# Hybrid encoder block on one core: pooling's products as the mixer's first projections, value convolutions between the retention heads, z gates behind them

## Chip, cores, metric

One core of a Trainium2 chip. The metric is the device time of one launch in microseconds; several runs of a kernel give a median. The engines are TensorE (PE in the rows; PEld is its weight load), VectorE (DVE), ScalarE (ACT), GpSimd (POOL) and SyncE (SP, which issues the weight transfers).

## What is computed

Two layers, each a token mixer and a SwiGLU feed-forward, on 512 tokens of width 1024. The mixer projects the normalised input and feeds three branches:

```python
qkv = silu(causal_depthwise_conv(dn_qkv, dn_conv))          # q, k, v of the delta rule, 4 heads
o_dn = gated_delta_rule(l2(q), l2(k), v, beta, g)           # chunks of 64, state carried over 8 chunks
o_dn = rms(o_dn) * dn_out_norm * silu(dn_z)                 # the z gate
o_pool = einsum(trailing_mean(u, (2, 4, 8, 16)) - u, pool_w) * pool_scale
o_ret = group_norm(chunkwise_retention(rq, rk, rv)) * ret_out_norm * silu(ret_g)
y = gate0 * (o_dn @ w_branch_dn) + gate1 * (o_pool @ w_branch_pool) + gate2 * (o_ret @ w_branch_ret)
x = x + rms_norm(y @ w_out);  then the feed-forward
```

`g` and `beta` (the token gates) come from a narrow projection of eight columns.

## The kernel before

Activations lie transposed: 128 channels on the partitions, 512 tokens along the row. Every float32 product is made from rounded halves: `weights` loads a 128 x 1024 weight block by SP, `split1` cuts each half of it into a high part on ACT (L232, `wh`) and a low part on DVE (L233, `wl`), and `mm3` (L222 to L224) adds three matmuls. A projection (`project`) is thus 24 matmuls of 512 columns, and a branch product of `w_branch_*` 12. The input norm's factor `rb` is not known when the first products of a stage run, so each projection's result is multiplied by `rb` when it leaves PSUM.

At a stage's start four projections run while the stage before is being finished (`begin`, `hand_over`); which four is said by `first_of_mixer`: in the kernel before the four key projections. Their PSUM tiles are the list `firsts`.

The mixer itself consists of one long chain and of filler. The chain is `delta()`: token gates (L505 to L570; its matmuls are L514, L520 and L567), transposed keys (L689), decays from GpSimd sums (L709, L710, matmuls L717, L718), Gram matrices (L737, L740), a forward solve of 15 small DVE steps, two block levels (`back`), eight chunk steps that carry the state (L800, L815, L837), norm and output. The filler is the list `tasks`: generators that each give one projection or branch product in pieces; whenever the chain yields n, `fill(n)` runs n pieces of the first task and a piece of `side` (retention's `attention`). `need(key)` runs tasks until a convolution is there.

A framework then orders each engine's instructions by its own estimate of when they are ready, so that the order below is what counts, not the order of the code. Each engine works its list in order.

Task order before: convolutions of the four keys from `firsts`; `pooled` 0 to 3, each with its projection; query convolutions with `pool_map` and the first two branch products of pooling (`p(0)`, `p(1)`) between them; each value convolution with one `p(n)`; retention heads 0 and 1, `p(6)`, heads 2 and 3, `p(7)`; eight branch products of retention. The z gates' projections are run by the chain itself at its end (L858). The branch of the delta rule and `w_out` follow in the tail.

`pooled(gi)` multiplies the projection by `rb` on DVE (L959, tile `u`), then adds shifted copies on GpSimd (L965; gi + 1 adds for window 2 to the power gi + 1, ten in all), and subtracts on DVE (L969, L973, L976). Its tiles, like those of the convolutions, gates and the retention, come from one tag `ft` of four buffers:

```python
        def ft():
            return tl("ft", FT, (P, S + 16))
```

Of the kernel before, what the change touches and what calls it, by code (L numbers as in the profile page):

```python
# [9 lines left out]
F32 = mybir.dt.float32  # L10
F32R = mybir.dt.float32r
# [7 lines left out]
P = 128  # L19
# [113 lines left out]
def tile_hybrid(ctx: ExitStack, tc: tile.TileContext, x_in, consts, rot, rmask, vecs, wab, wi, wpl, wbr, wo, wgu, wd, out):  # L133
# [325 lines left out]
        return dst, hs, rb, pss  # L459

    def first_of_mixer(l):
        return vec[:, l, V_PRE1 : V_PRE1 + KT], [wi[l, B_K + h] for h in range(H)]

    def first_of_ffn(l):
        return vec[:, l, V_PRE2 : V_PRE2 + KT], [wgu[l, 0, 0], wgu[l, 0, 1], wgu[l, 1, 0], wgu[l, 1, 1]]
# [15 lines left out]
    def mixer(l, xd, hs, rb, firsts):  # L481
# [17 lines left out]


        tok = {}

        def token_gates():
            raw = tl("mc", 2, (P, NT * B16))
            nc.scalar.dma_start(out=raw, in_=wab[l])  # L505
            abw = keep.tile([P, D], F32R, tag="wq", bufs=H, name=nm("abw"))
            G.memset(abw.bitcast(F32), 0.0)
            r8, w8 = raw.rearrange("p (k n) -> p k n", n=8), abw.rearrange("p (k n) -> p k n", n=P)
            V.tensor_copy(out=w8[:, :, 0:8], in_=r8)
            V.tensor_tensor(out=w8[:, :, 8:16], in0=r8, in1=w8[:, :, 0:8].bitcast(F32), op=ALU.subtract)  # L510
            ps = psum_f()
            for k in range(KT):
                for j in range(2):
                    T.matmul(ps, lhsT=w8[:, k], rhs=hs[k][j], start=k == 0 and j == 0, stop=k == KT - 1 and j == 1)  # L514
            yield
            ab = tl("ft", FT, (P, S + 16))
            V.tensor_tensor(out=ab[0:16, 0:S], in0=ps[0:16], in1=rb[0:16], op=ALU.mult)
            pst = psum_o()
            for t in range(NT):
                T.matmul(  # L520
                    pst[:, t * 8 : t * 8 + 8], lhsT=ab[0:16, ts(t)], rhs=kc[0:16, K_SEL : K_SEL + 8], start=True, stop=True
                )
            yield
            abt = pst[:, 0:32].rearrange("p (t n) -> p n t", n=8)

            beta = tiny("beta")
            A.activation(out=beta.rearrange("p (n t) -> p n t", n=4), in_=abt[:, 0:4], func=AF.Sigmoid)
            sx = tiny("sx")
            V.tensor_tensor(
                out=sx.rearrange("p (n t) -> p n t", n=4),  # L530
                in0=abt[:, 4:8],
                in1=vec[:, l, V_DTB : V_DTB + 16].rearrange("p (n t) -> p n t", n=4),
                op=ALU.add,
            )

            nab = tiny("nab")
            V.scalar_tensor_tensor(out=nab, in0=sx, scalar=-1.0, in1=sx, op0=ALU.mult, op1=ALU.min)
            e = tiny("e")
            A.activation(out=e, in_=nab, func=AF.Exp)
            ea = tiny("ea")  # L540
            A.activation(out=ea, in_=vec[:, l, V_ALOG : V_ALOG + 16], func=AF.Exp)
            den = tiny("den")
            V.tensor_scalar(out=den, in0=e, scalar1=2.0, scalar2=None, op0=ALU.add)
            V.reciprocal(out=den, in_=den)
            yield
            z = tiny("z")
            V.tensor_tensor(out=z, in0=e, in1=den, op=ALU.mult)
            z2 = tiny("z2")
            V.tensor_tensor(out=z2, in0=z, in1=z, op=ALU.mult)
            po = tl("po", 2, (P, 16))  # L550
            V.tensor_scalar(out=po, in0=z2, scalar1=2.0 / 17, scalar2=None, op0=ALU.mult)
            for c in (15, 13, 11, 9, 7, 5, 3):
                po2 = tl("po", 2, (P, 16))
                V.scalar_tensor_tensor(out=po2, in0=po, scalar=2.0 / c, in1=z2, op0=ALU.add, op1=ALU.mult)
                po = po2
            yield
            lp = tiny("lp")
            V.scalar_tensor_tensor(out=lp, in0=po, scalar=2.0, in1=z, op0=ALU.add, op1=ALU.mult)
            sp = tiny("sp")
            V.scalar_tensor_tensor(out=sp, in0=sx, scalar=0.0, in1=lp, op0=ALU.max, op1=ALU.add)  # L560
            g = tiny("g")
            V.scalar_tensor_tensor(out=g, in0=sp, scalar=-1.0, in1=ea, op0=ALU.mult, op1=ALU.mult)
            for _ in range(GATES):
                yield
            pcs = psum_c()
            for n, m in enumerate((c_le, c_gt, c_e0, c_e1)):
                T.matmul(pcs[:, n * 16 : n * 16 + 16], lhsT=m, rhs=g, start=True, stop=True)  # L567
            yield
            ex = tiny("ex", 64)
            A.activation(out=ex, in_=pcs[:, 0:64], func=AF.Exp)  # L570
            tok.update(beta=beta, g=g, e_g=ex[:, 0:16], e_tail=ex[:, 16:32], e_last=[ex[:, 32:48], ex[:, 48:64]])
            yield
# [1 line left out]

        wq = [keep.tile([P, 3 * S], F32, tag="wq", bufs=H, name=nm("wq")) for _ in range(H)]
        w4 = [t.rearrange("p (t s c) -> p t s c", t=NT, s=6) for t in wq]

        ku = tl("ku", 1, (P, H * S))  # L580
        k4 = ku.rearrange("p (h t v) -> p h t v", h=H, t=NT)
# [59 lines left out]
                done.add(key)  # L641
                yield

        def conv_first():
            for h, ps_ in enumerate(firsts):
                conv(ps_, 4 + h, ("k", h))
                yield

        def z_gate(h):
            res = []  # L650
            yield from project(wi[l, B_Z + h], hs, res)
            t = tl("ft", FT, (P, S + 16))[:, 0:S]
            V.tensor_tensor(out=t, in0=res[0], in1=rb, op=ALU.mult)
            sg = tl("ft", FT, (P, S + 16))[:, 0:S]
            A.activation(out=sg, in_=t, func=AF.Sigmoid)
            o = tl("c1", 4)
            V.scalar_tensor_tensor(out=o, in0=t, scalar=vec[:, l, V_DN : V_DN + 1], in1=sg, op0=ALU.mult, op1=ALU.mult)
            return o

        def square_sums(src, v, h):  # L660
            sq = tl("c1", 4)
# [12 lines left out]
                V.tensor_copy(out=out[ROWS[f]], in_=src[ROWS[1 - f]])  # L674
            return out

        os_ = []

        def delta():
            half = (P, NT * C)  # L680
# [174 lines left out]
            V.tensor_tensor(out=rt, in0=r, in1=rqw, op=ALU.mult)  # L855
            yield WAITS["norm"]
            for h in range(H):
                zg = yield from z_gate(h)  # L858
                on = tl("c1", 4)
                scaled(on, hs_of(ku, h), rt[:, hc(h)])  # L860
                yield WAITS["on"]
                ps = psum_c()
                transposed(on, ps)
                od = tl("ft", FT, (P, S + 16))[:, 0:S]
                for f in range(2):
                    a, b = slice(f * C, (f + 1) * C), slice((1 - f) * C, (2 - f) * C)
                    V.tensor_tensor(out=hd(od)[:, :, a], in0=hd(ps)[:, :, b], in1=hd(zg)[:, :, a], op=ALU.mult)
                os = keep.tile([P, 2 * S], F32R, tag="wq", bufs=H, name=nm("os"))
                split1(od, os[:, 0:S], os[:, S:])
                os_.append((os[:, 0:S], os[:, S:]))  # L870
# [80 lines left out]
        mixes = {}  # L951

        def pooled(gi):
            res = []
            yield from project(wi[l, B_PU + gi], hs, res)
            win, pad = 2 ** (gi + 1), 16
            u = ft()
            G.memset(u[:, 0:pad], 0.0)
            V.tensor_tensor(out=u[:, pad:], in0=res[0], in1=rb, op=ALU.mult)  # L959
            src, first = u, 0  # L960
            for a in range(gi + 1):
                d = 2**a
                first += d
                t = ft()
                G.tensor_tensor(out=t[:, first:], in0=src[:, first:], in1=src[:, first - d : S + pad - d], op=ALU.add)  # L965
                src = t
            tag = ("kr", "qr", "vc", "mask")[gi]
            mixed = tl(tag)
            V.scalar_tensor_tensor(  # L969
                out=mixed[:, 16:], in0=src[:, pad + 16 :], scalar=1.0 / win, in1=u[:, pad + 16 :], op0=ALU.mult, op1=ALU.subtract  # L970
            )
            t = tl("pc", 1, (P, 16))
            V.tensor_tensor(  # L973
                out=t, in0=src[:, pad : pad + 16], in1=kc[:, K_CNT + 16 * gi : K_CNT + 16 * gi + 16], op=ALU.mult
            )
            V.tensor_tensor(out=mixed[:, 0:16], in0=t, in1=u[:, pad : pad + 16], op=ALU.subtract)  # L976
            mixes[gi] = mixed
            yield

        def pool_map(gi):  # L980
            mixed = mixes[gi]
# [134 lines left out]
            return [branch(i, name, gb, n) for n in range(a, b)]  # L1116

        def convs(what, h):
            b, ch = {"q": (B_Q, 0), "v": (B_V, 8)}[what]
            return [conv_one(b + h, ch + h, (what, h))]  # L1120

        def p(n):
            return branches(0, "p", B_GA + 8, n, n + 1)

        side = []
        tasks = [conv_first()] + [pooled(i) for i in range(4)]
        tasks += convs("q", 0) + [pool_map(0), pool_map(1)] + convs("q", 1) + [pool_map(2), pool_map(3)]
        tasks += convs("q", 2) + p(0) + convs("q", 3) + p(1)
        for h in range(H):
            tasks += convs("v", h) + p(2 + h)  # L1130
        tasks += [retention(0), retention(1)] + p(6) + [retention(2), retention(3)] + p(7)
        tasks += branches(1, "r", B_GA + 16, 0, 8)

        def fill(n):
# [230 lines left out]
```

## Time and profile before

| | |
|---|---|
| median of 3 runs | 1900.73 us (1898.32 to 1903.97) |
| the profiled execution | 1900.81 us, span 1898.9 us |
| granted clock, mean over the span | 0.987 of 2.4 GHz |
| PE busy | 1834.2 us (97%) |
| DVE / ACT / POOL busy | 1041.6 (55%) / 701.0 (37%) / 395.4 us (21%) |
| chain that ended last | PE 82%, DVE 12%, ACT 2% |

Busy time of a matmul on PE overlaps that of the next. The engine lines tell how much of the span an engine worked; the 40 slices and the view by stretches tell where it did not; the timeline says of each gap on PE which engine's instruction ended it. Where PE has nothing else to do, a gap on PE is time.

### The profile page before, as it was taken

The page shows a single profiled execution, that of the slowest core. Times are in us where ns is not written, and L with a number is a line of the kernel's source. Part 1 is how long each engine was busy: PE and PEld are TensorE (multiplying, and loading weights), DVE is VectorE, ACT ScalarE, POOL GpSimd, SP SyncE. Part 2 cuts the span into 40 slices and gives each one's busy share as a digit, 9 for nine tenths or more (in the row PEclk, how much of TensorE's full clock was granted, in tenths as well). Part 3 has the DMA queues.
Part 4 walks back from the last instruction along what each step waited for, and adds up shares of the span by engine and source line. Part 5 has one row for each costly group of instructions (what it writes and reads, how often), then busy time and mean ns, then how long its engine had stood idle before and what let it go on. Part 6 is the DMA issues. An engine that isn't in the chain of part 4 may idle for free.

```text
span 1898.9 us, 24790 instructions
## 1 busy us (share of the span) xinstructions
PE 1834.2 (97%) x9286; PEld 1537.4 (81%) x9286; DVE 1041.6 (55%) x1973; ACT 701.0 (37%) x1251; POOL 395.4 (21%) x370
## 2 busy tenths in 40 slices
PE   7899999999999999999998999999999999999997
PEld 6677888778888888888976788887788988888887
DVE  6886476654438432343487965766544474324443
ACT  5533333233344332333354333332333443323332
POOL 2602010111223220222226020011122232102212
PEclk9899999999999999999998999999999999999999
DMA  6131112224325333223231211222243252333231
GB/s 203 45 95 59 56 59 81 92 79 144 99 67 182 98 100 100 93 96 100 79 129 45 85 58 59 66 81 92 78 144 100 78 178 91 98 100 99 91 100 45
DMA packets 65415, 177.70 MB, mean 94 GB/s; under 512 B 15376, under 2 KB 18448, under 8 KB 65296
## 3 DMA queue, kind: packets, MB, share of 16 engines
q1 hardware_dynamic: 54016, 172.78, 27.9%
q10 hardware_dynamic: 11280, 3.34, 0.8%
q8 instruction: 73, 1.20, 0.3%
q14 instruction: 46, 0.38, 0.1%
HBM read 167.18 MB, written 8.39 MB: 92 GB/s over the span
## 4 chain that ended last, share of the span: by engine, by line
PE 82%; DVE 12%; ACT 2%; issue 2%; ACTq 1%; DMA 1%; POOL 1%; SPq 0%; DVEq 0%; POOLq 0%
PE pp L222 24%; PE pp L223 24%; PE pp L224 24%; DVE wl L233 2%; DVE ct L610 1%; ACTq L782 1%; DVE hl L229 1%; PE cx L815 1%; PE cx L898 1%; DVE xt L329 1%; PE cx L908 1%; PE cx L800 1%; PE fx L498 1%; PE fx L267 1%; PE cx L498 0%
## 5 line engine op out<-in xcount | busy, mean ns | idle before, releaser
L232 ACT ACTIVATE wh<-raw 128x512 fp32r<-128x512 f32 x584 | 364.5, 628 | 726.7 <-PE pp L223 677.9
L222 PE MATMUL pp<-hh,wh 128*128 128x512 f32 x1568 | 624.1, 398 | 0.0
L223 PE MATMUL pp<-hl,wh 128*128 128x512 f32 x1568 | 615.5, 393 | 0.0
L224 PE MATMUL pp<-hh,wl 128*128 128x512 f32 x1568 | 614.0, 392 | 0.0
L233 DVE TENSOR_TENSOR wl<-raw,wh 128x512 fp32r<-128x512 f32 x584 | 416.3, 716 | 328.0 <-ACT wh L232 310.2
L222 PEld LDWEIGHTS pp<-hh,wh 128*128 128x128 f32 x1568 | 296.2, 189 | 62.6 <-issue 2.5
L224 PEld LDWEIGHTS pp<-hh,wl 128*128 128x128 f32 x1568 | 295.6, 189 | 62.2 <-issue 0.3
L223 PEld LDWEIGHTS pp<-hl,wh 128*128 128x128 f32 x1568 | 296.2, 189 | 59.6 <-issue 1.5
L222 PE MATMUL pp<-ah,wh 128*128 128x512 f32 (+1 forms) x418 | 149.1, 357 | 0.0
L224 PE MATMUL pp<-ah,wl 128*128 128x512 f32 (+1 forms) x418 | 148.6, 356 | 0.0
L223 PE MATMUL pp<-al,wh 128*128 128x512 f32 (+1 forms) x418 | 148.5, 356 | 0.0
L1244 POOL TENSOR_TENSOR gs<-gt,sg 128x512 f32<-128x512 f32 x44 | 56.6, 1287 | 314.3 <-ACT sg L1242 314.3
L1249 POOL TENSOR_TENSOR a<-gs,ut 128x512 f32<-128x512 f32 x44 | 70.4, 1601 | 135.9 <-DVE ut L1247 135.6
L289 POOL TENSOR_TENSOR sqa<-sqa,sq 128x256 f32<-128x256 f32 (+1 forms) x69 | 62.6, 907 | 127.4 <-ACT sq L282 108.1
L224 PEld LDWEIGHTS pp<-ah,wl 128*128 128x128 f32 x418 | 78.9, 189 | 11.4
L222 PEld LDWEIGHTS pp<-ah,wh 128*128 128x128 f32 x418 | 78.9, 189 | 11.4
L223 PEld LDWEIGHTS pp<-al,wh 128*128 128x128 f32 x418 | 79.0, 189 | 11.2
L233 DVE TENSOR_TENSOR al<-a,ah 128x512 fp32r<-128x512 f32 x44 | 31.3, 711 | 77.7 <-ACT ah L232 77.5
L610 DVE SCALAR_TENSOR_TENSOR ct<-ft,vec,ct 128x512 f32<-128x512 f32 x72 | 58.3, 810 | 9.0 <-ACT ct L607 7.9
L222 PE MATMUL pp<-yh,wh 128*128 128x256 f32 (+1 forms) x192 | 61.4, 320 | 0.0
L1247 DVE TENSOR_TENSOR ut<-pp,rb 128x512 f32<-128x512 f32 x42 | 29.0, 690 | 58.7 <-PE pp L224 58.7
L224 PE MATMUL pp<-yh,wl 128*128 128x256 f32 (+1 forms) x192 | 61.1, 318 | 0.0
(297 smaller groups left out, 2382.4 us busy)
## 6 DMA issues: line engine op xcount, KB each, us to landing
raw<-in_wi_dram SPq DMA_DIRECT2D x117, 512.0 KB
raw<-in_wgu_dram SPq DMA_DIRECT2D x88, 512.0 KB
raw<-in_wd_dram SPq DMA_DIRECT2D x44, 512.0 KB
raw<-in_wbr_dram SPq DMA_DIRECT2D x24, 512.0 KB
raw<-in_wo_dram SPq DMA_DIRECT2D x16, 512.0 KB
xd<-xt SPq DMA_DIRECT2D x24, 256.0 KB
xt<-xd SPq DMA_DIRECT2D x24, 256.0 KB
xt<-in_x_dram SPq DMA_DIRECT2D x16, 256.0 KB
```

The lines of the kernel that those rows point to most:

```text
L222: T.matmul(ps, lhsT=w[0], rhs=m[0], start=start, stop=False)
L223: T.matmul(ps, lhsT=w[0], rhs=m[1], start=False, stop=False)
L224: T.matmul(ps, lhsT=w[1], rhs=m[0], start=False, stop=stop)
L229: V.scalar_tensor_tensor(out=lo, in0=src, scalar=scalar, in1=hi.bitcast(F32), op0=ALU.mult, op1=ALU.subtract)
L232: A.activation(out=hi, in_=src, func=AF.Copy)
L233: V.tensor_tensor(out=lo, in0=src, in1=hi.bitcast(F32), op=ALU.subtract)
L267: T.matmul(ps[:, t : t + 1], lhsT=sq[:, ts(t)], rhs=one, start=i == 0, stop=i == len(sqs) - 1)
L289: G.tensor_tensor(out=t, in0=acc[0], in1=acc[1], op=ALU.add)
L610: V.scalar_tensor_tensor(out=a2, in0=u[:, j : j + S], scalar=tap(j), in1=a, op0=ALU.mult, op1=ALU.add)
L1244: G.tensor_tensor(out=gs, in0=gt, in1=sg, op=ALU.mult)
L1247: V.tensor_tensor(out=ut, in0=up, in1=rb, op=ALU.mult)
L1249: G.tensor_tensor(out=a, in0=gs, in1=ut, op=ALU.mult)
```

## The change

`first_of_mixer` names the four pooling projections, and `pooled` becomes a plain function that takes them from `firsts` and runs four times before the tasks begin. Keys are projected and convolved as tasks, `pool_map` and the eight branch products of pooling stand between key and query convolutions (the last one behind the first value convolution), and the value convolutions stand between the retention heads. The z gates become tasks behind the retention; their outputs are kept in four buffers that are free by then, and the chain waits for them by `need`. The tile `abw` is taken first from its tag, and the four `wq` tiles when they are first used. No arithmetic is changed.

```diff
     def first_of_mixer(l):
-        return vec[:, l, V_PRE1 : V_PRE1 + KT], [wi[l, B_K + h] for h in range(H)]
+        return vec[:, l, V_PRE1 : V_PRE1 + KT], [wi[l, B_PU + g] for g in range(4)]
...
         tok = {}
+        abw = keep.tile([P, D], F32R, tag="wq", bufs=H, name=nm("abw"))
...
-            abw = keep.tile([P, D], F32R, tag="wq", bufs=H, name=nm("abw"))
...
-        def conv_first():
-            for h, ps_ in enumerate(firsts):
-                conv(ps_, 4 + h, ("k", h))
-                yield
...
-            o = tl("c1", 4)
+            o = tl(("cv", "crb", "srb", "kr")[h])
             V.scalar_tensor_tensor(out=o, in0=t, scalar=vec[:, l, V_DN : V_DN + 1], in1=sg, op0=ALU.mult, op1=ALU.mult)
-            return o
+            zg[h] = o
+            done.add(("z", h))
+            yield
...
             for h in range(H):
-                zg = yield from z_gate(h)
+                need(("z", h))
...
         def pooled(gi):
-            res = []
-            yield from project(wi[l, B_PU + gi], hs, res)
             win, pad = 2 ** (gi + 1), 16
             u = ft()
             G.memset(u[:, 0:pad], 0.0)
-            V.tensor_tensor(out=u[:, pad:], in0=res[0], in1=rb, op=ALU.mult)
+            V.tensor_tensor(out=u[:, pad:], in0=firsts[gi], in1=rb, op=ALU.mult)
...
         side = []
-        tasks = [conv_first()] + [pooled(i) for i in range(4)]
-        tasks += convs("q", 0) + [pool_map(0), pool_map(1)] + convs("q", 1) + [pool_map(2), pool_map(3)]
-        tasks += convs("q", 2) + p(0) + convs("q", 3) + p(1)
+        for i in range(4):
+            pooled(i)
+        tasks = convs("k", 0) + [pool_map(0), pool_map(1)] + convs("k", 1) + [pool_map(2), pool_map(3)]
+        tasks += p(0) + convs("k", 2) + p(1) + convs("k", 3) + p(2)
         for h in range(H):
-            tasks += convs("v", h) + p(2 + h)
-        tasks += [retention(0), retention(1)] + p(6) + [retention(2), retention(3)] + p(7)
+            tasks += convs("q", h) + p(3 + h)
+        tasks += convs("v", 0) + p(7)
+        for h in range(H):
+            tasks += [retention(h)] + (convs("v", h + 1) if h + 1 < H else [])
+        tasks += [z_gate(h) for h in range(H)]
         tasks += branches(1, "r", B_GA + 16, 0, 8)
```

What the built program makes of it is shown at three places.

**The start of the first mixer.** On DVE of the kernel before, the first rows behind the stage change: the key convolution's multiply by `rb` (L600) and taps (L610), then L517, which takes the token gates' projection out of PSUM.

```order
L600 TENSOR_TENSOR ft_384<-cx_128,rb_127 128x512 [waits Activation_49]
L233 TENSOR_TENSOR wl_743<-raw_711,wh_742 128x512 [waits PE_49,Activation_49]
L610 SCALAR_TENSOR_TENSOR ct_389<-ft_384,vec,ct_387 128x512 [waits Activation_49]
L610 SCALAR_TENSOR_TENSOR ct_391<-ft_384,vec,ct_389 128x512 [waits DVE_49]
L610 SCALAR_TENSOR_TENSOR ct_393<-ft_384,vec,ct_391 128x512 [waits DVE_49]
L517 TENSOR_TENSOR ft_398<-fx_367,rb_127 16x512 [waits PE_49]
L600 TENSOR_TENSOR ft_405<-cx_129,rb_127 128x512
```

The same place on DVE of the changed kernel, from the third pooling group's subtraction ahead of L517 (`vc`) to the fourth's (`mask`); ahead of these stand the first two groups (`kr`, `qr`).

```order
L969 SCALAR_TENSOR_TENSOR qr_375<-ft_373,ft_368 128x496 [waits Pool_49]
L973 TENSOR_TENSOR pc_377<-ft_373,kc 128x16 [waits DVE_49]
L959 TENSOR_TENSOR ft_380<-cx_130,rb_127 128x512
L976 TENSOR_TENSOR qr_375<-pc_377,ft_368 128x16 [waits DVE_49]
L959 TENSOR_TENSOR ft_394<-pp_271,rb_127 128x512 [waits Pool_49]
L969 SCALAR_TENSOR_TENSOR vc_389<-ft_387,ft_380 128x496 [waits Pool_49]
L973 TENSOR_TENSOR pc_391<-ft_387,kc 128x16 [waits DVE_49]
L976 TENSOR_TENSOR vc_389<-pc_391,ft_380 128x16 [waits DVE_49]
L233 TENSOR_TENSOR wl_708<-raw_688,wh_707 128x512 [waits PE_49,Activation_49]
L517 TENSOR_TENSOR ft_445<-fx_415,rb_127 16x512 [waits Pool_49]
L969 SCALAR_TENSOR_TENSOR mask_405<-ft_403,ft_394 128x496 [waits Pool_49]
```

L517 stood behind one key convolution and waited for PE; it now stands behind three pooling groups and waits for POOL (the buffer of its output is that of the fourth group's second add, free when the third add, `ft_401`, has read it). On PE, L520, the next matmul of the token gates, stood four matmuls behind the last L514; it now stands behind 21, the key projection of head 0:

```order
L222 MATMUL pp_434<-hh_123,wh_471 128x512
L223 MATMUL pp_434<-hl_124,wh_471 128x512
L224 MATMUL pp_434<-hh_123,wl_472 128x512
L520 MATMUL fx_447<-kc,ft_445 128x8 x4
L222 MATMUL pp_434<-hh_125,wh_471 128x512
L223 MATMUL pp_434<-hl_126,wh_471 128x512
L224 MATMUL pp_434<-hh_125,wl_472 128x512
L982 MATMUL fx_528<-kr_363,sw_350 128x512
```

**The end of the retention, on PE of the first mixer.** Before, the transposes of the last head's normed output (L498, `fx_3597`) stand directly ahead of the first branch product that needs it (`oh_3604`):

```order
L222 MATMUL pp_3580<-hh_125,wh_3608 128x512
L223 MATMUL pp_3580<-hl_126,wh_3608 128x512
L224 MATMUL pp_3580<-hh_125,wl_3609 128x512
L498 MATMUL fx_3597<-kc,ft_3547 128x128 x4
L222 MATMUL pp_3630<-oh_2558,wh_3631 128x512
L223 MATMUL pp_3630<-ol_2559,wh_3631 128x512
```

In the changed kernel the same transposes (`fx_3354`) stand inside the projection of the second z gate (`pp_3307`):

```order
L223 MATMUL pp_3307<-hl_122,wh_3344 128x512
L224 MATMUL pp_3307<-hh_121,wl_3345 128x512
L498 MATMUL fx_3354<-kc,ft_3281 128x128 x4
L222 MATMUL pp_3307<-hh_123,wh_3344 128x512
L223 MATMUL pp_3307<-hl_124,wh_3344 128x512
```

Six more matmuls of that projection, two further z projections and a gate now stand between them and the first branch product of retention.

**The start of the chunk steps, on PE of the first mixer.** In the changed kernel the first state product (L817, L815 before) and the next step's product with that state (L802, L800 before) are four matmuls apart, inside the query projection of retention head 3 (`pp_2975`); before, twelve stood there.

```order
L817 MATMUL cx_2931<-ku_349,wq_853 128x128
L223 MATMUL pp_2975<-hl_120,wh_3012 128x512
L224 MATMUL pp_2975<-hh_119,wl_3013 128x512
L222 MATMUL pp_2975<-hh_121,wh_3012 128x512
L223 MATMUL pp_2975<-hl_122,wh_3012 128x512
L802 MATMUL cx_2961<-uu_2936,wq_520 128x128
L802 MATMUL cx_2961<-uu_2936,wq_605 128x128
```

Two more gaps of three or four matmuls follow; from the second step on twelve stand between, as before.

## Rows read from the trace of the kernel before

**Rows 1.** The page, part 1: busy time and share of the span.

```profile
PE 1834.2 (97%) x9286; PEld 1537.4 (81%) x9286; DVE 1041.6 (55%) x1973; ACT 701.0 (37%) x1251; POOL 395.4 (21%) x370
```

**Rows 2.** By stretches: start:end, length, busy per engine, clock, DMA share, GB/s.

```profile
35.00:100.00 65.00, 58.44 (x259) 46.19 (x258) 54.30 (x101) 33.68 (x51) 33.74 (x44) 0.92 0.16 49
975.00:1040.00 65.00, 54.14 (x214) 42.59 (x213) 49.44 (x96) 31.86 (x49) 32.64 (x42) 0.87 0.17 57
300.00:400.00 100.00, 95.68 (x456) 78.07 (x455) 67.12 (x131) 33.24 (x56) 9.34 (x6) 0.98 0.26 81
390.00:400.00 10.00, 7.66 (x29) 5.77 (x28) 7.27 (x19) 3.29 (x6) 0.00 (x0) 0.83 0.00 2
```

**Rows 3.** Timeline of PE, start of mixer 1: start, length, [idle before <-releaser].

```profile
42.73 1.02 PE L520 MATMUL fx<-kc,ft 16*128 16x8 f32 x8 [0.68 <-DVE ft L517]
...
61.95 1.89 PE L567 MATMUL cx<-g,kc 128*128 128x16 f32 x8 [2.52 <-DVE g L562]
...
80.95 0.70 PE L717 MATMUL cx<-c,kc 128*128 128x256 f32 x2 [2.98 <-POOL c L709]
```

**Rows 4.** The same view, start of mixer 2.

```profile
979.77 0.57 PE L514 MATMUL fx<-hh,abw 128*128 128x512 f32 x1 [2.40 <-DVE abw L510]
...
1007.55 1.89 PE L567 MATMUL cx<-g,kc 128*128 128x16 f32 x8 [3.17 <-DVE g L562]
...
1021.65 1.22 PE L717 MATMUL cx<-c,kc 128*128 128x256 f32 x2 [3.05 <-POOL c L709]
...
1031.37 0.70 PE L717 MATMUL cx<-c,kc 128*128 128x256 f32 x2 [1.22 <-POOL c L709]
...
1033.08 0.70 PE L718 MATMUL cx<-c,kc 128*128 128x256 f32 x2 [1.01 <-POOL c L710]
```

**Rows 5.** The same view, end of the retention in mixer 1.

```profile
350.29 0.94 PE L1076 MATMUL fx<-vc,ft 128*128 128x128 f32 x6 [0.94 <-ACT ft L1071]
...
371.65 0.63 PE L498 MATMUL fx<-kc,ft 128*128 128x128 f32 x4 [0.83 <-DVE ft L1035]
...
394.86 0.66 PE L498 MATMUL fx<-kc,ft 128*128 128x128 f32 x4 [2.34 <-DVE ft L494]
```

**Rows 6.** Line L965, pooling's adds on GpSimd: shortest/median/longest in ns.

```profile
L965 POOL TENSOR_TENSOR ft<-ft x20: 1053/1384/2042, 50.1 to 1019.2; 128x527 f32<-128x527 f32 x8, 128x525 f32<-128x525 f32 x6, 128x521 f32<-128x521 f32 x4, 128x513 f32<-128x513 f32 x2
```

**Rows 7.** Timeline of POOL: the rotary table's multiply, mixers 1 and 2.

```profile
38.08 1.79 POOL L1009 TENSOR_TENSOR srb<-srb,rb 128x512 f32<-128x512 f32 x1
...
978.28 1.27 POOL L1009 TENSOR_TENSOR srb<-srb,rb 128x512 f32<-128x512 f32 x1
```

**Rows 8.** DVE lines: two by line, two groups of 30:130 (count, busy, mean ns).

```profile
L959 DVE TENSOR_TENSOR ft<-pp,rb x8: 678/685/692, 48.6 to 1014.5; 128x512 f32<-128x512 f32 x8
...
L969 DVE SCALAR_TENSOR_TENSOR kr<-ft,ft x2: 676/676/677, 51.6 to 994.5; 128x496 f32<-128x496 f32 x2
...
L973 DVE TENSOR_TENSOR pc<-ft,kc 128x16 f32<-128x16 f32 x4 | 0.7, 165 | 0.0
...
L610 DVE SCALAR_TENSOR_TENSOR ct<-ft,vec,ct 128x512 f32<-128x512 f32 x24 | 20.6, 857 | 0.8 <-ACT ct L607 0.5
```

**Rows 9.** Timeline of PE: product starts, and two `pool_map` products in the chain.

```profile
40.98 0.39 PE L222 MATMUL pp<-hh,wh 128*128 128x512 f32 x1
...
41.66 0.39 PE L222 MATMUL pp<-hh,wh 128*128 128x512 f32 x1
...
985.11 0.39 PE L224 MATMUL pp<-hh,wl 128*128 128x512 f32 x1
...
88.07 1.72 PE fx L983 x4
```

**Rows 10.** A table load on ACT, and PE's waits for convolution outputs (total, times, longest).

```profile
50.02 1.28 ACT L613 ACT_TABLE_LOAD   x1 [1.02 <-DVE ct L610]
...
PE cx L737 <- DVE wq L621: 0.8, 2, 0.4
```

More of the change, by code (lines that the diff above doesn't have):

```diff
@@ L572, in token_gates, with __missing__ @@
             yield
-        wq = [keep.tile([P, 3 * S], F32, tag="wq", bufs=H, name=nm("wq")) for _ in range(H)]
-        w4 = [t.rearrange("p (t s c) -> p t s c", t=NT, s=6) for t in wq]
+        class on_demand(dict):
+            def __missing__(self, h):
+                wq = keep.tile([P, 3 * S], F32, tag="wq", bufs=H, name=nm("wq"))
+                self[h] = wq.rearrange("p (t s c) -> p t s c", t=NT, s=6)
+                return self[h]
+        w4 = on_demand()
         ku = tl("ku", 1, (P, H * S))
@@ L675, in swapped @@
             return out
-        os_ = []
+        os_, zg = [], {}
         def delta():
@@ L866, in delta @@
                     a, b = slice(f * C, (f + 1) * C), slice((1 - f) * C, (2 - f) * C)
-                    V.tensor_tensor(out=hd(od)[:, :, a], in0=hd(ps)[:, :, b], in1=hd(zg)[:, :, a], op=ALU.mult)
+                    V.tensor_tensor(out=hd(od)[:, :, a], in0=hd(ps)[:, :, b], in1=hd(zg[h])[:, :, a], op=ALU.mult)
                 os = keep.tile([P, 2 * S], F32R, tag="wq", bufs=H, name=nm("os"))
@@ L977, in pooled @@
             mixes[gi] = mixed
-            yield
         def pool_map(gi):
@@ L1118, in convs @@
         def convs(what, h):
-            b, ch = {"q": (B_Q, 0), "v": (B_V, 8)}[what]
+            b, ch = {"q": (B_Q, 0), "k": (B_K, 4), "v": (B_V, 8)}[what]
             return [conv_one(b + h, ch + h, (what, h))]
```

## The prediction

> **What bounds the kernel now.** I read the page first, then the view by stretches, then the timeline of PE and, for each gap, the engine that ended it. PE works 97% of the span [rows 1], and the order of the tasks takes no matmul away. What an order can give back is PE's idle time, and the time in which its granted clock is down because it was idle. In the two mixers both lie in few places.
>
> At the start of mixer 1 PE waits 0.68 us at L520, 2.52 us at L567 and 2.98 us at L717 [rows 3], 6.2 us together. The clock of that stretch is 0.92 over 65 us [rows 2]: 0.08 x 65 = 5.2 us of work lost. At the start of mixer 2 there are five waits, 2.40 + 3.17 + 3.05 + 1.22 + 1.01 = 10.85 us [rows 4], and clock 0.87 over 65 us [rows 2], so 0.13 x 65 = 8.45 us. The waits at L567 end when DVE has the log-decay g, the last of a chain of small operations; those at L717 and L718 end when POOL has its decay sums, which stand behind pooling's adds. DVE is busy 54.3 of the first 65 us.
>
> At the end of the retention, PE waits 0.94, 0.83 and 2.34 us [rows 5]; behind the last the clock is 0.83 for 10 us [rows 2], 1.7 us lost. Mixer 2 has the same three waits to 0.01 us, without the drop. Sum: 5.8 and 4.1 us. The bill of before is thus 11.4 + 19.3 + 5.8 + 4.1 = **40.6 us**, of 1900.8. A few waits of below 1.4 us between block levels stay as they are, since their order stays, and are left out on both sides.
>
> **The change, part by part.**
>
> *Keys leave the first four projections, pooling takes them.* The number of matmuls, transfers and DVE operations stays. SP issues the same weight blocks in another order. ACT gets eight more table loads of 1.28 us [rows 10], 10 us, since sigmoids now alternate with exponentials; ACT works 37% [rows 1] and the loads stand beside projections, so I cost them at nothing; a load ahead of a copy that PE waits for would cost its 1.28 us.
>
> *The new wait: L520.* This is the price. Four pooling groups now start at once when `rb` is there, and the token gates stand behind three of them on DVE, and by a buffer behind POOL's ninth add. The chain for mixer 1, in the time of before: POOL ends the rotary multiply at 38.08 + 1.79 = 39.87 [rows 7]. Then nine adds [rows 6], three short memsets (0.1 each, an estimate; below the 0.165 of L973), and between the second and third group POOL waits for DVE: L969 0.68, L973 0.17, L959 0.69 [rows 8]; at last L517, as wide as L959. An add takes between 1.05 and a median of 1.38. I take 1.2: nearer the shortest, since during this chain DVE mostly waits for POOL instead of working beside it. L517 then ends at 39.87 + 10.8 + 0.3 + 1.54 + 0.7 = 53.2. PE is there earlier: the last L514 ends at 40.98, a matmul every 0.68 / 3 = 0.227 [rows 9], 21 of them: 45.75. **Wait 7.5 us** (6.1 with the shortest add, 9.1 with the median), where it was 0.68.
>
> In mixer 2 POOL is free at 979.55 [rows 7], L517 ends at 992.9; PE is done with L514 at 985.1 [rows 9] and has 22 products ahead, so it arrives at 990.1: **wait 2.8 us** (1.4 to 4.4). The wait at L514 for `abw`, 2.40 us, stays: it hangs on a transfer that is not moved.
>
> Queued behind L517 on DVE is the whole token-gate chain. From it to g there are 15 wide operations (10.8 us at 0.68 to 0.77) and 18 small ones (3.1 us at 0.17), 13.9 us; PE meanwhile has L520 with 1.0, 42 products (9.5) and four `pool_map` products of 0.86 (two take 1.72 [rows 9]; 3.4), 13.9 us too, and more while the clock is low. POOL has no adds left there, so the small operations should not be stretched. In mixer 2 it is 16.2 against 15.3 us. So the wait at L567 goes to about nothing, with 2.5 and 3.2 us, as before, as its upper end.
>
> *Clock.* The gaps of over 2.3 us are followed by a loss: 5.2 us for two gaps, 8.45 for three, 1.7 for one. I take 2.6 us behind each L520, with 1.7 and 3.4 (twice that) as ends; for mixer 2's short gap the lower end is zero. Behind L514 the loss stays; I take the smallest of these, 1.7.
>
> *Decay sums.* L711 (L709 before) now comes 8.5 projections after the stage start instead of four, and POOL has finished pooling by then. The waits at L717 and L718 go.
>
> *Keys as tasks.* PE's transposes of each key head now stand behind that head's convolution. The nearest row is PE's wait for the same kind of output at L737, 0.4 at the longest [rows 10]: zero to 1.6 us a mixer, I take 0.5.
>
> *z gates behind the retention.* More than two projections (over 11 us) now stand between the last head's transposes and the product that needs them, where nothing stood. The waits of rows 5 go; I leave 0.5 us a mixer for the copy at L1071.
>
> *Thinner cover in the first chunk steps.* Three gaps there hold three or four matmuls (0.7 to 0.9 us) instead of twelve. The nearest row is a wait of 0.94 us for an ACT copy of a product [rows 5]; zero to 0.94 for each gap, I take half: 1.5 us a mixer.
>
> **Sum.** After: mixer 1 start 7.5 + 2.6 = 10.1; mixer 2 start 2.4 + 1.7 + 2.8 + 2.6 = 9.5; keys 1.0, retention's end 1.0, thin cover 3.0: 24.6 us. Gain 40.6 - 24.6 = 16.0 us, so 1900.8 - 16.0 = **1884.8 us**. The profiled execution, 1900.81, is the median of the runs to 0.1 us, so it needs no correction. With every new cost at its lower end (6.1 + 1.7; 2.4 + 1.7 + 1.4; nothing else) 13.3 us are left: 1873.5.
>
> *A rule that speaks against it.* The rows of L965 spread from 1.05 to 2.04 us for the same work. The Trainium skill, "SBUF — State Buffer", section "SBUF: two separate sides", says that a VectorE operation with two SBUF inputs and a GpSimd operation lock each other out for their whole length. By it the subtractions of three groups (0.68 + 0.17 + 0.17 each) would stand in line with the nine shortest adds, L517 would end at 54.1, the first wait would be 8.3 us, and the gain some 15 us. The spread of the rows agrees with such a lock.
>
> **Rivals.**
>
> *No change: the wait only moves.* Adds at the median, the larger clock loss, and L567 waiting as long as before with its own loss: 9.1 + 3.4 + 2.5 + 3.4 = 18.4 and 2.4 + 1.7 + 4.4 + 3.4 + 3.2 + 3.4 = 18.5, with the 5.0 of the other parts 41.9 us against 40.6: **1902**. For it: all the gates still hang on one chain of small DVE operations, and PE's and DVE's shares behind L517 are equal to the tenth. Against it: DVE has four key convolutions less in that stretch.
>
> *Slower: POOL's chain becomes the stage.* If DVE and POOL hold each other up so that an add takes 2.04 us, the longest of rows 6, L517 ends at 60.8 and 1000.5; PE waits 15.0 and 10.4 us, and L567 waits behind it as above. 24.3 + 24.5 + 5.0 = 53.8 us, 13.2 more than before: **1914**. It decides from an "after" of 46 us on, which is an add of 1.6 us on the mean. For it: the ten adds stand back to back now. Against it: half the rows are below 1.38 though DVE was busy 84% of that time.
>
> *Faster still:* below 1874 only if DVE and POOL overlap better than any row shows.
>
> **How the numbers follow.** A difference of 0.3%, 5.7 us, is about what a measurement of this kernel can tell from none. The forecast (1874 to 1895) has 0.68, no change 0.18, slower 0.11, still faster 0.03. The range is 1873 to 1903: it leaves out the slower rival and the tail of the fast one. Faster by over 0.3% (below 1895): 0.70, from the forecast and the still faster case, less a little for the forecast's upper edge. Within: 0.18; slower: 0.12.
>
> **What would show it.** In the changed kernel's timeline: PE's largest wait at L520 <- DVE L517, 6 to 9 us in mixer 1 and 1 to 4 in mixer 2, with POOL's L965 back to back before it; no wait above 1 us at L719 (L717 before); nothing above 1 us between the last head's transposes and retention's branch; L567 below 1 us. The clock of mixer 2's first 65 us rises from 0.87 to about 0.93. I am wrong if L520 waits above 10 us in mixer 1, if L567 keeps its 2.5 to 3.2, or if new waits of together over 5 us stand between the value convolutions and the chunk steps, where DVE's work has been packed closer.

## The result, and the profile after

The changed kernel takes **1882.12 us** (median of 4 runs, 1880.23 to 1883.61). The kernel before took 1900.89 us in 4 runs on the same chip. The ratio of the two is 0.9905, with a 95% interval of 0.9892 to 0.9919: faster by 18.8 us between the medians, by 18 us by the ratio. The forecast was 1884.8 us and a gain of 16.

The page of the changed kernel, parts 1 and 2 (rows 1 hold the line of before):

```profile
span 1881.4 us, 24775 instructions
...
PE 1825.2 (97%) x9286; PEld 1532.4 (81%) x9286; DVE 1037.3 (55%) x1973; ACT 712.8 (38%) x1259; POOL 397.2 (21%) x370
```

The span fell by 17.5 us (before: 1898.9). PE does the same 9286 matmuls. It is busy 9.0 us less [rows 1], and so idle 8.5 us less: a part of the gain is waits, and the other is, by the clock of the stretches below, matmuls that no longer run at the lower clock. ACT's eight more table loads of 1.28 us are 10.2 of its 11.8 us more; two of PE's waits at L739 hang on such loads, as the part on why the prediction was right shows.

What PE waited for in the whole run (engine, tile and line, what ended the wait: total us, times, longest); the first lines for mixers and hand-overs:

```profile
PE fx L520 <- DVE ft L517: 15.1, 2, 7.9
PE fx L275 <- DVE rsy L259: 10.3, 9, 2.5
...
PE cx L498 <- DVE uu L884: 2.6, 2, 1.3
...
PE fx L514 <- DVE abw L510: 2.3, 1, 2.3
PE cx L739 <- DVE wq L626: 2.2, 4, 1.1
...
PE cx L900 <- ACT c L902: 1.7, 2, 0.9
PE fx L498 <- DVE cv L622: 1.1, 3, 0.4
PE cx L691 <- DVE wq L626: 0.9, 3, 0.3
```

L567, L719 (L717 before) and the end of the retention (L1075 and the transposes L498 of `ft`) have no line any more: rows 3, 4 and 5 are gone, but for L514 and L520. In their place stands one kind of wait, twice. The timeline of PE, [idle before <-releaser]:

```profile
53.60 1.84 PE L520 MATMUL fx<-kc,ft 16*128 16x8 f32 x8 [7.94 <-DVE ft L517]
...
973.89 0.47 PE L514 MATMUL fx<-hh,abw 128*128 128x512 f32 x1 [2.34 <-DVE abw L510]
...
989.90 1.84 PE L520 MATMUL fx<-kc,ft 16*128 16x8 f32 x8 [7.11 <-DVE ft L517]
```

By stretches (columns as in rows 2):

```profile
35.00:100.00 65.00, 56.84 (x243) 44.68 (x243) 40.05 (x79) 28.30 (x43) 17.67 (x22) 0.89 0.18 59
975.00:1040.00 65.00, 57.57 (x246) 45.15 (x245) 46.20 (x91) 29.61 (x46) 14.55 (x18) 0.92 0.23 76
300.00:400.00 100.00, 99.89 (x582) 82.67 (x581) 74.11 (x157) 39.85 (x83) 8.20 (x6) 1.00 0.19 64
53.60:62.20 8.60, 8.60 (x21) 5.84 (x22) 5.18 (x14) 3.83 (x7) 0.78 (x4) 0.54 0.00 2
989.90:997.40 7.50, 7.50 (x19) 5.15 (x20) 4.94 (x13) 2.98 (x6) 0.79 (x4) 0.54 0.00 0
```

The stretch 300:400 rose from 95.68 busy and clock 0.98 [rows 2] to 99.89 and 1.00. The clock of mixer 2's first 65 us rose from 0.87 to 0.92 (forecast about 0.93); that of mixer 1's fell from 0.92 to 0.89. Right behind each L520, PE is busy all the time but the granted clock is 0.54, nearly all of it at the lower of the two levels (1.2 GHz). The work lost is 0.46 x 8.6 = 4.0 us and 0.46 x 7.5 = 3.5 us. The price of the new wait is so 11.9 us in mixer 1 and 10.6 us in mixer 2.

How L517 comes to be so late is read from GpSimd and VectorE in mixer 1. First GpSimd, from the rotary multiply on:

```profile
37.84 1.29 POOL L1008 TENSOR_TENSOR srb<-srb,rb 128x512 f32<-128x512 f32 x1
39.09 1.07 POOL L965 TENSOR_TENSOR ft<-ft 128x527 f32<-128x527 f32 x1
...
44.88 3.33 POOL L965 TENSOR_TENSOR ft<-ft 128x527 f32<-128x527 f32 x3 [1.37 <-DVE qr L976]
48.16 0.11 POOL L958 MEMSET ft<- 128x16 f32 x1
48.35 1.50 POOL L965 TENSOR_TENSOR ft<-ft 128x527 f32<-128x527 f32 x1
50.02 4.06 POOL L965 TENSOR_TENSOR ft<-ft 128x525 f32<-128x525 f32 x3 [0.18 <-DVE pc L973]
```

Then VectorE over the last part of the same time:

```profile
48.25 0.68 DVE L969 SCALAR_TENSOR_TENSOR vc<-ft,ft 128x496 f32<-128x496 f32 x1 [0.44 <-POOL ft L965]
48.84 1.04 DVE L973 TENSOR_TENSOR pc<-ft,kc 128x16 f32<-128x16 f32 x1
49.91 0.18 DVE L976 TENSOR_TENSOR vc<-pc,ft 128x16 f32<-128x16 f32 x1
50.01 0.68 DVE L233 TENSOR_TENSOR wl<-raw,wh 128x512 fp32r<-128x512 f32 x1
52.77 0.68 DVE L517 TENSOR_TENSOR ft<-fx,rb 16x512 f32<-16x512 f32 x1 [2.08 <-POOL ft L965]
```

VectorE is idle for 2.08 us ahead of L517 and waits for an add of GpSimd: the `ft` buffer of the forecast. L973, a multiply of 16 columns, takes 1.04 us beside an add, where the trace of before has 165 ns [rows 8].

### The profile page after: what moved, and what is told of

It is laid out like the page before. It is cut to its first block, busy times and chain, and to the rows that moved or that the text cites. A ratio compares the mean times of both kernels' runs of the same rounds, so it can differ in the third digit from the quotient of the medians.

```text
span 1881.4 us, 24775 instructions
## 1 busy us (share of the span) xinstructions
PE 1825.2 (97%) x9286; PEld 1532.4 (81%) x9286; DVE 1037.3 (55%) x1973; ACT 712.8 (38%) x1259; POOL 397.2 (21%) x370
## 4 chain that ended last, share of the span: by engine, by line
PE 83%; DVE 9%; ACT 3%; issue 2%; ACTq 1%; DMA 1%; POOL 1%; SPq 0%; DVEq 0%; POOLq 0%
PE pp L222 24%; PE pp L224 24%; PE pp L223 24%; DVE wl L233 2%; DVE ct L615 1%; DVE hl L229 1%; ACTq L784 1%; PE cx L817 1%; PE cx L910 1%; DVE xt L329 1%; PE cx L900 1%; POOL ft L965 1%; DMA raw<-in_wi_dram 1%; PE fx L498 1%; PE cx L802 1%
## 5 line engine op out<-in xcount | busy, mean ns | idle before, releaser
L233 DVE TENSOR_TENSOR wl<-raw,wh 128x512 fp32r<-128x512 f32 x584 | 423.7, 728 | 324.6 <-ACT wh L232 309.6
L1002 POOL TENSOR_TENSOR y<-y,ft 128x512 f32<-128x512 f32 x16 | 26.0, 1623 | 179.2 <-DVE ft L1001 179.2
L615 DVE SCALAR_TENSOR_TENSOR ct<-ft,vec,ct 128x512 f32<-128x512 f32 x72 | 55.4, 770 | 12.0 <-ACT ct L612 10.6
L232 ACT ACTIVATE ah<-a 128x512 fp32r<-128x512 f32 x44 | 27.8, 632 | 89.2 <-POOL a L1252 89.2
```

Source lines behind the costliest of these rows:

```text
L232: A.activation(out=hi, in_=src, func=AF.Copy)
L233: V.tensor_tensor(out=lo, in0=src, in1=hi.bitcast(F32), op=ALU.subtract)
L615: V.scalar_tensor_tensor(out=a2, in0=u[:, j : j + S], scalar=tap(j), in1=a, op0=ALU.mult, op1=ALU.add)
L1002: G.tensor_tensor(out=ys[n], in0=ys[n], in1=t, op=ALU.add)
```

## Experiments

Theory: the gain is the waits at L567, at the decay sums and at the retention's end with their clock; what is given back is the wait at L520, made by pooling's add chain and the `ft` buffer. Each run stands beside runs of the kernel before, whose median lay between 1897.77 and 1900.21. None stands beside runs of the changed kernel, so a difference of some 3 us from its 1882.12 tells little.

**The z gates alone.** The kernel before, plus this part of the change:

```diff
-            o = tl("c1", 4)
+            o = tl(("cv", "crb", "srb", "kr")[h])
...
-                zg = yield from z_gate(h)
+                need(("z", h))
...
+        tasks += [z_gate(h) for h in range(H)]
         tasks += branches(1, "r", B_GA + 16, 0, 8)
```

> The kernel before with one part of the change alone: the four z gates become tasks behind the retention heads instead of steps inside the chain. My theory: it takes away the two stretches of waits at the end of the retention (5.8 and 4.1 us, with a little clock) and nothing at the start of the mixers, so about 1891 us, 1889 to 1894; the waits at the decay sums, at L567 and at L514 of the kernel before stay (about 11 us behind L717 to L718, L567 and L514 in the two mixers). Rival: the z gates are the whole gain and the start of the mixers only swaps one wait for another of the same size, then about 1882 us. Second rival: the retention's end was hidden or is given back later, then 1900 us.

Measured 1892.5 us (1890.66 to 1895.83), ratio 0.996 (0.9946 to 0.9974): the time expected, but not by the steps expected. In the stretch 380:400 PE is now busy throughout (columns as in rows 2):

```profile
380.00:400.00 20.00, 20.00 (x91) 16.50 (x90) 11.87 (x20) 7.38 (x12) 1.67 (x1) 1.00 0.32 106
```

But the end of the retention now lies some 25 us earlier, and the three waits of rows 5 are still there. Only the last is shorter, 1.00 instead of 2.34 us:

```profile
324.81 0.94 PE L1078 MATMUL fx<-vc,ft 128*128 128x128 f32 x6 [0.93 <-ACT ft L1073]
...
346.13 0.63 PE L498 MATMUL fx<-kc,ft 128*128 128x128 f32 x4 [0.83 <-DVE ft L1037]
...
369.29 0.66 PE L498 MATMUL fx<-kc,ft 128*128 128x128 f32 x4 [1.00 <-DVE ft L494]
```

Mixer 2 has the same three, and each mixer a new one of 0.4 us. So 1.9 us of waits are gone, and the drop of the clock behind the last one in mixer 1 (1.00 from 369.3 to 380.0; 1.7 us lost before). That is 3.6 of the 7.7 us between the medians; for the others this trace, of the slowest of the five runs, has no row. PE's waits at the mixers' starts stay: 9.3 us at L719 and 5.7 us at L567. About 8 of the 18 us come with the z gates; the rest is put down to the mixers' start.

**Value convolutions in a row.** The changed kernel, with them ahead of the retention:

```diff
-        tasks += convs("v", 0) + p(7)
         for h in range(H):
-            tasks += [retention(h)] + (convs("v", h + 1) if h + 1 < H else [])
+            tasks += convs("v", h)
+        tasks += p(7) + [retention(h) for h in range(H)]
```

> The changed kernel, but with its four value convolutions in a row ahead of the retention, not between its heads. My theory counts the convolutions between heads at nothing, so the time stays at 1882 us, 1880 to 1884, and no wait of over 1 us appears at the value convolutions. Rival: spreading them is what removed the waits at the retention (VectorE and ScalarE bunch up behind four convolutions in a row), then 1886 us or more, with waits at L498 or L567 in that stretch.

Measured 1882.79 us (1881.38 to 1883.86): the same. Where the value convolutions stand is worth nothing in time here. Yet 3.9 us of waits, none above 0.94, are back in the retention (L1067, L1075, L498): together with the run before this shows that it is not the z gates alone that clear the retention of waits.

**A buffer of its own for L517's output.**

```diff
-            ab = tl("ft", FT, (P, S + 16))
+            ab = tl("c1", 4)
```

> The changed kernel, with the output of L517 in a buffer of another pool tag (c1), so that it need not wait for GpSimd's ninth pooling add to give back an ft buffer. VectorE's order stays. My theory: L517 starts where its queue lets it, behind the third group's last small operation, about 2.1 us earlier in both mixers; the waits at L520 go from 7.94 and 7.11 us to about 5.9 and 5.0, and with a little of the clock 1877 us, 1875 to 1879. Rival: VectorE's order alone sets it (the buffer came free no later than the queue), then 1882 us and 7.9 and 7.1 us as before.

Measured 1875.03 us (1872.21 to 1876.39), the time expected, but not by the steps expected. The order did not stay. With another buffer the framework put L517 ahead of the third pooling group on VectorE (it starts at 44.56 instead of 52.77) and L520 seven rows behind the last L514 on PE, where it was 22. The timeline of PE shows what that gives:

```profile
45.37 1.02 PE L520 MATMUL fx<-kc,c 16*128 16x8 f32 x8 [3.30 <-DVE c L517]
62.24 1.06 PE L567 MATMUL cx<-g,kc 128*128 128x16 f32 x8 [2.94 <-DVE g L562]
...
979.71 1.02 PE L520 MATMUL fx<-kc,c 16*128 16x8 f32 x8 [0.71 <-DVE c L517]
985.52 1.77 PE L982 MATMUL fx<-qr,sw 128*128 128x512 f32 x2 [2.34 <-DVE sx L529]
```

Of the 15.1 us at L520, 4.0 are left, but 5.3 us of new waits stand at L567 and L982.

**Pooling's groups as tasks between the steps of the token gates**, with that buffer:

```diff
+        def pooled_task(i):
+            pooled(i)
+            yield
...
-        for i in range(4):
-            pooled(i)
-        tasks = convs("k", 0) + [pool_map(0), pool_map(1)] + convs("k", 1) + [pool_map(2), pool_map(3)]
+        tasks = [pooled_task(i) for i in range(4)] + convs("k", 0) + [pool_map(0), pool_map(1)] + convs("k", 1) + [pool_map(2), pool_map(3)]
```

> As the run with the buffer of its own, and pooling's four groups are issued one by one as tasks between the steps of the token gates, so that L517 stands behind two groups on VectorE and not behind three and a ninth add. My theory: L517 then starts within 1 us of TensorE's last token-gate product (L514), the wait at L520 falls under 1.5 us in both mixers, the clock does not fall there, and the time is 1866 us, 1861 to 1872. Rival: the steps behind it (sigmoid, the decay's polynomial, L567) only take over the wait, since the chain of small operations is the bound of the mixer's start, then 1876 to 1882 us, with new waits at L567, L717 or L718. Second rival: TensorE waits for the pooling maps (late groups three and four), 1 to 4 us at L983.

Measured 1875.69 us (1874.24 to 1876.43): a miss by 10 us. The first rival came in its place, 0.3 us below its range. L517 starts at 44.54, no earlier than with the buffer alone, since VectorE has it behind the same operations. Waits of 4.1 us at L520 (3.76 of it in mixer 1), 2.3 at L982 and 2.6 at L567 (two together) remain.

**Rotary multiplies behind the pooling groups.** In the code the two multiplies of `crb` and `srb` move from L1008 to behind the loop over `pooled`.

> The changed kernel, with GpSimd's two multiplies of the rotary tables (1.29 us each ahead of the first pooling add) issued behind the pooling groups. My theory: GpSimd's adds are the chain that L517 ends up behind, and the first add could start with the end of the first group's multiply, about 1.9 us earlier in mixer 1 and up to 1 us in mixer 2; the waits at L520 go from 7.9 and 7.1 us to about 6 and 6.5, and the time to 1879 us, 1877 to 1881. Rival: the chain's start is not what counts (the second group's multiply, late behind a weight split, sets the pace), then 1882 us.

Measured 1881.38 us (1879.05 to 1882.89), with 7.95 and 7.15 us at L520. This tells nothing of the theory: GpSimd's list was the same again, as its timeline shows (L1127 is where the multiply now stands in the code):

```profile
37.59 1.30 POOL L1127 TENSOR_TENSOR srb<-srb,rb 128x512 f32<-128x512 f32 x1
38.84 1.07 POOL L965 TENSOR_TENSOR ft<-ft 128x527 f32<-128x527 f32 x1
```

What an earlier start of the adds would be worth stays open.

**Task steps under the wait.**

```diff
             V.tensor_tensor(out=ab[0:16, 0:S], in0=ps[0:16], in1=rb[0:16], op=ALU.mult)
+            yield 4
             pst = psum_o()
```

> The changed kernel, with four steps of the tasks (key convolutions' products, about 5.4 us at 24 products of 0.227 us for four) handed to TensorE between L517 and the products at L520 that wait for it. VectorE's and GpSimd's order of the pooling is not touched. My theory: the wait at L520 is latency that other products can stand in for; it falls to about 2.5 and 1.7 us, the clock stays up for longer, and the time is 1870 us, 1866 to 1875. Rival: the steps are only taken from under a later wait, which then shows (L567, L717, L982), and the time is 1878 to 1882 us.

Measured 1878.25 us (1875.14 to 1879.88), the rival's time; the ratio's interval, 0.9863 to 0.9904, overlaps that of the changed kernel. Of the four steps only five more matmuls came to stand ahead of L520 in mixer 1; the framework pulled it forward again. The waits are 6.42 and 3.20 us, and the one at L514 grew from 2.34 to 4.55 us.

**Both edits together.**

> Both: the buffer of its own for L517's output, and the four task steps ahead of L520. The run with the buffer alone showed that L517 moved ahead of the third pooling group, waits of 3.30 and 0.71 us at L520, and new ones at L982 (2.3) and L567 (2.9). My theory: the steps cover both waits at L520 and the one at L982, and 1870 us comes out, 1867 to 1874. Rival: the small operations behind L520 are now the bound, and since the steps delay them too, the wait at L567 grows by 1 to 3 us and the time stays at 1875 us.

Measured 1876.51 us (1875.99 to 1878.02), no better than the buffer alone. It is the rival's time, but not its way: L567 does not wait. L520 no longer waits in mixer 1, and the wait stands one product further on, at the pooling maps (line numbers are one higher):

```profile
56.47 2.08 PE L983 MATMUL fx<-qr,sw 128*128 128x512 f32 x2 [7.34 <-DVE ol L229]
```

So the cover moved the wait to the next product that hangs on VectorE.

**Pooling's adds on VectorE.** The changed kernel, with

```diff
-                G.tensor_tensor(out=t[:, first:], in0=src[:, first:], in1=src[:, first - d : S + pad - d], op=ALU.add)
+                V.tensor_tensor(out=t[:, first:], in0=src[:, first:], in1=src[:, first - d : S + pad - d], op=ALU.add)
```

> The changed kernel, with pooling's ten adds per mixer on VectorE instead of GpSimd. My theory: the price of the wait at L520 is the add chain at 1.05 to 1.6 us an add with a hand-over each way, while the two engines hold each other up; at VectorE's 0.68 us for such an operation the third group and the ninth add end some 3 us earlier, the waits at L520 are 4 to 5 us in both mixers, VectorE's 165 ns operations never take 1.03 us, and the time is 1876 us, 1872 to 1879. Rival: VectorE, now with ten more operations in line, delays the weight splits at its end, TensorE waits at the convolutions' weights instead and the time is 1881 us or more.

Measured **1862.46 us** (1857.92 to 1863.01), ratio to before 0.9801 (0.9782 to 0.982): some 20 us below the changed kernel, where 6 were expected. The direction was right and the worth too small by a factor of three. The line of its adds, and its stretches (columns as in rows 2):

```profile
L965 DVE TENSOR_TENSOR ft<-ft x20: 674/693/1181, 35.4 to 972.2; 128x527 f32<-128x527 f32 x8, 128x525 f32<-128x525 f32 x6, 128x521 f32<-128x521 f32 x4, 128x513 f32<-128x513 f32 x2
```

```profile
35.00:100.00 65.00, 63.96 (x289) 51.22 (x288) 51.84 (x112) 33.85 (x52) 7.59 (x16) 1.00 0.25 79
...
975.00:1040.00 65.00, 64.68 (x302) 51.86 (x302) 48.82 (x98) 42.30 (x62) 18.87 (x28) 1.00 0.24 76
```

An add takes 0.69 us against a median of 1.31 in the changed kernel. PE's only wait in mixer 1's start is 0.72 us at L520, mixer 2 has none at L520, and the clock is 1.00 in both. In mixer 1 L517 starts 4.1 us earlier (48.65) and PE reaches L520 3.1 us later (48.75 instead of 45.66), since it now stands 44 rows behind the last L514 instead of 22: 7.2 of the 7.94 us. So 3.1 us come from an order that the expectation did not have. The waits at L520 (15.1 to 0.7 us) and the clock that no longer falls behind them (4.0 and 3.5 us) are together 21.9 us, enough for the whole difference.

**The same, with the buffer of its own.**

> The changed kernel with the adds on VectorE and with a buffer of its own for L517's output. By the framework's estimates L520 now stands 15 rows behind L514's last product on TensorE in mixer 1 (44 with the adds alone on VectorE, 22 in the changed kernel). My theory: how far L520 stands behind L514 in TensorE's list counts as much as when L517 ends; with only 15 rows of cover a wait of 2 to 3 us comes back at L520, and the time is 1866 us, 1862 to 1870. Rival: an earlier L517 is all that matters, then no wait is left and 1860 us or less.

Measured 1859.47 us (1858.23 to 1862.62). My theory fell: with 15 rows of cover no wait of 2 to 3 us came, but 0.78 us, since L517 ended as early as 42.7. The two kernels with VectorE's adds can't be told apart; both are faster than before and after.

**The kernel before with the adds on VectorE**, and nothing else:

> The kernel before, with pooling's ten adds per mixer on VectorE instead of GpSimd and nothing else. My theory: there the adds stand between the decay sums and the first products of the state on GpSimd, so the waits at L717 to L719 shrink by some 3 us a mixer, while L567 and L514 wait as before and the retention's end keeps its 5.8 and 4.1 us: 1892 us, 1886 to 1898. So the change, with the adds on VectorE as well (1862 us), would be worth far more than without it. Rival: GpSimd's adds were the whole trouble of the kernel before too, and with them on VectorE it runs at 1875 us or less, so that the reordering itself is worth little.

Measured 1881.3 us (1878.42 to 1882.61): 18 us off, twice what I expected, between theory and rival, and as much as the whole change. PE's waits at L717 and L718 fall from 8.7 to 1.6 us, and the 5.7 us at L567 vanish, although VectorE has more to do; those at L737 grow from 0.8 to 5.4 us. In the kernel before, adds run ahead of g, and operations of VectorE beside them are stretched. Three rows of its timeline there, two of mixer 1 and one of mixer 2, where the same operations otherwise take 0.17, 0.68 and 0.17 us:

```profile
56.45 1.04 DVE L554 SCALAR_TENSOR_TENSOR po<-po,z 128x16 f32<-128x16 f32 x1
...
58.99 1.55 DVE L233 TENSOR_TENSOR wl<-raw,wh 128x512 fp32r<-128x512 f32 x1
...
1006.44 1.06 DVE L562 SCALAR_TENSOR_TENSOR g<-sp,ea 128x16 f32<-128x16 f32 x1
```

In mixer 2 four operations of 16 columns on the way to g take 0.93 to 1.06 us there, together 3.4 us more than alone. With the adds on VectorE g ends 3.1 us earlier behind L517's start (19.1 instead of 22.2 us), which is nearly all of the 3.17 us at L567 [rows 4]. In mixer 1, g ends only 0.4 us earlier (19.6 instead of 20.0 us); most of the 2.52 us [rows 3] is gone because 77 instead of 68 matmuls now stand between L520 and L567 (9 x 0.227 = 2.0 us). Over the stretch 35:100 the means (the number behind the comma) fall too. Before:

```profile
L233 DVE TENSOR_TENSOR wl<-raw,wh 128x512 fp32r<-128x512 f32 x13 | 10.6, 814 | 1.4 <-ACT wh L232 1.4
...
L554 DVE SCALAR_TENSOR_TENSOR po<-po,z 128x16 f32<-128x16 f32 x7 | 2.0, 293 | 0.0
```

With the adds on VectorE:

```profile
L233 DVE TENSOR_TENSOR wl<-raw,wh 128x512 fp32r<-128x512 f32 x15 | 10.1, 682 | 1.4 <-ACT wh L232 1.4
...
L554 DVE SCALAR_TENSOR_TENSOR po<-po,z 128x16 f32<-128x16 f32 x7 | 1.2, 166 | 0.0
```

By the ratios, reordering and moving the adds are worth 18 us each alone, and 38 together.

## Why the prediction was right

The total and the main mechanism held: the old waits go, and one new wait at L520, with its clock, gives part of it back. Three steps did not: L520 in mixer 2, the chain to g, and the table loads.

*The bill of before*: of its 40.6 us, the waits at L567, at the decay sums and at the retention's end are gone in the trace. The reason given for the retention's end, the z gates behind it, is not the whole of it. The z gates alone came to 7.7 us where 8.9 were forecast (9.9 less 1.0), but left 2.8 of the 4.1 us of waits a mixer.

*L520 in mixer 1*: 7.5 forecast, 7.94 measured. L517 ended at 53.45 against 53.2. The adds came to about 1.3 us instead of 1.2, and the multiplies ahead of them were done 0.7 us earlier.

*L520 in mixer 2* is the term that was mis-sized: 2.8 forecast, 7.11 measured, above its upper end of 4.4. Two steps failed. The chain from L514's start to L517's end took 15.9 us, not 13.1. Of these 2.8 us, 1.25 are GpSimd's wait for the second `u`, which comes late behind a weight split of 1.57 us on VectorE, and 1.3 are the nine adds, 1.34 us on the mean instead of 1.2. The stretched L973, 1.03 us where I had 0.17, held GpSimd up by 0.18 us twice. And PE arrived 8.9 us behind the start of L514, not 10.3, because the clock did not fall behind that wait. The 1.7 us booked there for the clock were not lost. The split, the second `u` and the add that waits for it:

```profile
973.67 1.57 DVE L233 TENSOR_TENSOR wl<-raw,wh 128x512 fp32r<-128x512 f32 x1
975.16 0.68 DVE L959 TENSOR_TENSOR ft<-cx,rb 128x512 f32<-128x512 f32 x1
...
975.98 1.36 POOL L965 TENSOR_TENSOR ft<-ft 128x527 f32<-128x527 f32 x1 [1.25 <-DVE ft L959]
```

*Clock behind L520*: 2.6 us each forecast, 4.0 and 3.5 measured, a little above the upper end of 3.4. The two starts cost 11.9 + 2.3 + 10.6 = 24.8 us by the trace, 19.6 by the forecast.

*What made up for it*: thinner cover in the first chunk steps, 3.0 us, cost nothing (L498 of `uu` 2.6 against 2.3 us before, L900 1.7 against 2.5), nor did the end of the retention (1.0). Keys as tasks, 1.0, show as 0.9 us at L691.

*Table loads*, booked at nothing, did cost. At the query heads' L739 PE waits 2.2 us, against 0.8 before (L737 [rows 10]). Its two longest waits there, 1.14 us in mixer 1 and 0.59 in mixer 2, each end a chain in which ACT loads a table for 1.28 us ahead of the convolution's sigmoid (L618), while VectorE idles 0.84 us until that sigmoid is there and only then makes PE's operand (L626). So some 0.84 and 0.59 us of them are the loads' price, an estimate from these rows. In mixer 1:

```profile
138.99 1.28 ACT L618 ACT_TABLE_LOAD   x1 [1.25 <-DVE ct L615]
...
141.69 0.66 PE L739 MATMUL cx<-kc,wq 128*128 128x128 f32 x4 [1.14 <-DVE wq L626]
```

So the two starts cost 5.2 us and L739 1.4 us more than forecast, and the terms for cover 4.0 us less. Summed by these rows the gain is about 13.5 us. Smaller waits that fell outside the bill, half of them at the stage changes, add 2.5; for some 1.5 us of the measured 17.5 I have no row. The total came out closer than its terms because their errors cancel, which is luck.

*L567 and the decay sums*: both to nothing, as forecast, but L567 by a margin of 0.3 us in mixer 1 (g ends at 71.18, PE comes at 71.50) and 0.2 in mixer 2. From L517's end to g's end it took 17.7 and 18.8 us where 13.9 and 16.2 were forecast, part of it waiting for PE's products. PE, forecast at 13.9 and 15.3 us, was 4.0 and 3.5 us slower by its clock, and so came no earlier than g. That the forecast wait of nothing came out is in part luck: with the buffer of its own, where less is lost at L520, L567 waits 2.94 us in mixer 1. The kernel before with VectorE's adds shows besides that taking the adds off GpSimd removes both old waits at L567, with the keys where they were.

*The rule*. The lock of "SBUF — State Buffer", section "SBUF: two separate sides", in the Trainium skill gave L517's end as 54.1, the sum without it 53.2; measured was 53.45. The trace agrees with a lock in that operations of 16 columns take 1.03 us beside an add, and end 0.03 us behind it (L973: 48.84 + 1.04 = 49.88, the add: 48.35 + 1.50 = 49.85). I weighed it for the new wait alone. The runs with the adds on VectorE show that what GpSimd's adds cost elsewhere is as large; how much of that is stretched operations, how much the shorter add and how much the order that follows from it, they don't separate.

*Rivals*. "No change" needed L567 to keep its wait; it did not, by the thin margin above. "Slower" needed adds of 1.6 us on the mean; they were 1.3.

## What to carry over

Where a short operation on VectorE feeds the chain that TensorE waits for, count the GpSimd work that runs beside it, by the longest row of the short operation, not by its mean; moving ten adds a mixer to the busier engine was worth as much as reordering the whole mixer. A scratch buffer out of a shared tag is a dependency on whoever held it last, and where a framework sorts by estimates it decides the order too, so read the built order after each edit before you price it. A wait that is covered by other work is gone only if the work behind it was not late as well: look at the next product down the list.

## What was not expected of the hardware

A multiply of 16 columns on VectorE takes 0.17 us alone and 1.03 to 1.04 us beside a GpSimd add, and it ends 0.03 to 0.04 us behind that add; its mean over the first 65 us of mixer 1 is 604 ns in the changed kernel and 162 ns with the adds on VectorE:

```profile
L973 DVE TENSOR_TENSOR pc<-ft,kc 128x16 f32<-128x16 f32 x4 | 2.4, 604 | 0.0
```

```profile
L973 DVE TENSOR_TENSOR pc<-ft,kc 128x16 f32<-128x16 f32 x4 | 0.6, 162 | 0.0
```

The length of a wait alone did not decide what the clock did behind it. At L514 of mixer 2 it stayed up behind 2.34 us in the changed kernel (1.00 from 973.9 to 982.0) and fell behind 2.40 us before (0.84 from 979 to 990). It stayed up behind 3.53 us with VectorE's adds and the buffer of its own, and fell behind 3.16 us with pooling's groups as tasks; the stretch behind each, in this order:

```profile
961.20:970.00 8.80, 8.74 (x40) 6.83 (x41) 8.80 (x19) 2.01 (x3) 0.22 (x2) 1.00 0.19 62
```

```profile
971.20:979.00 7.80, 7.49 (x27) 5.79 (x28) 6.86 (x12) 0.07 (x1) 6.04 (x7) 0.78 0.22 69
```

Behind waits of over 7 us in the changed kernel it was down for most of the next 7.5 to 8.6 us of full work (0.54).
